# Weights beside the attention land in two half places of their own, and the local branch's table of distances holds 320 columns

## The chip, the cores and the metric

The kernel runs on one core of one Trainium2 chip. The metric is the device time of one execution in microseconds (us). The kernel before took 1309.75 us (median of 3 runs, 1309.35 to 1310.75).

The core's engines have the names that the profile gives them: PE is TensorE (matmuls; PEld is its weight loads), DVE is VectorE, ACT is ScalarE, POOL is GpSimd, and SP issues the DMAs. Every engine works through its own list of instructions in order and waits on semaphores.

## The reference

One decoder layer over 1024 tokens of width 1024, all in float32. A joint projection of x feeds two groups of heads side by side: four differential heads (two softmaxes of 64-wide queries and keys, the second subtracted with a factor, then an RMS norm) and eight heads of native sparse attention (NSA) over two key groups. Each NSA head adds three gated branches: compressed keys, selected blocks, and a local window of 512. The local branch is what the table of distances belongs to:

```
mask = (dist_i >= 0) & (dist_i < WINDOW) & (kpos >= 0)[None, :]
s = jnp.einsum('bqghd,bkgd->bqghk', q_blk, kblk) * scale
s = s - slopes[None, None, :, :, None] * dist[None, :, None, None, :]
p = masked_softmax(s, mask[None, :, None, None, :])
```

Sixteen blocks are selected of sixteen that there are, so the selected branch is plain causal attention. Behind the attention come the output projection, a layer norm, a SwiGLU feed-forward part (width 2816) and a second layer norm.

## The kernel before, in words

**Precision.** A float32 matrix is split into a rounded part hi and a rest lo (`split`, L79: ACT casts, DVE or POOL subtracts), and a product is three matmuls, hi*hi, hi*lo and lo*hi (`mm3`, L114).

**Stages.** First the keys and the compressed branch's inputs are projected, then the values, then attention runs in units, and beside it the remaining projections run as fillers. Then the output projection ends, and the feed-forward part takes the second half of the span, from about 700 us on. Its code is not touched, but for the pool in which a small tile of statistics lies (L1166).

**Units.** A unit is one block of 128 queries of a pair of NSA heads in one branch (`nsa_units`, L361; kind 0 is the selected branch together with the compressed one, kind 1 the local one) or of one differential head (`diff_units`, L430). Its front computes scores into a psS bank (L311, L312), adds the distances and takes the minimum on DVE (L318), exponentiates on ACT (L332) and scales on POOL (L397, L454). Its back transposes on PE (L351, L341), splits again on ACT and DVE, and multiplies by the values into psO (L412, L414, L467). A front writes into one or two of six t tiles, and they stay taken until the back has read them. Distances come from tables made once on POOL at the start (`masks`, L259): dsel for causal attention, dwin for the local window, dcmp for the compressed keys. A local unit has up to five blocks of keys, 640 columns, reduced in two parts of 320.

**Fillers.** `k_fill`, `q_fill` and `dv_fill` (L511 to L554) each load a weight, split it and run chains of matmuls into one of two psM banks; 24 matmuls of 512 columns make a chain for half of the tokens. A q chain then needs two q tiles of a ring of four, which come free when an earlier half's scores are done; k and v chains write into named slots. The weights sit in a ring of five tiles of 1024 columns (`w_tile`, L69). `load_split` (L85) takes a third tile of this ring for the raw weight. It loads it in two halves of 512 columns, ACT casts each half into hi, and POOL subtracts it into lo (L90, L91).

**Order.** All instructions are written down in the order of the phase table (L783): per phase its units, its fillers, how many units may be open before the oldest one's back is written (look), how fast the fillers are spread, and by how many places a back's priority is put behind (later). Fillers stand 2000 places behind (`FILL_LATER`, L29). A planner then fixes each engine's order: it takes what is ready by a simulated clock and has the best priority, and gives out tiles as they come free in that simulation. The engines follow the fixed order on the chip.

**The end of the attention.** When four blocks of a differential head are done, `finish` (L477) normalises them, transposes them (L486) and stores them to mix_d. The output projection of a row block loads its rows from mix_d (`out_start`, L575), so its second half waits for head 3's finish.

Of the kernel before, what the change touches and what calls it, by code (L numbers as in the profile page):

```python
# [37 lines left out]
def layer_kernel(ctx: ExitStack, tc: tile.TileContext, xT, x, w_t, w_vg, w_dv, lam_in, subln,  # L38
# [105 lines left out]
    with ExitStack() as ctx_a:  # L144
# [105 lines left out]
        dsel = pa.tile([P, 1024], F32, tag="dsel", name="dsel", bufs=1)  # L250
        dwin = pa.tile([P, 640], F32, tag="dwin", name="dwin", bufs=1)
        dcmp = pa.tile([P, NC + 56], F32, tag="dcmp", name="dcmp", bufs=1)
# [6 lines left out]
        def masks():  # L259
# [3 lines left out]
                                    compare_op=ALU.is_ge, fill=BIG)  # L263
            nc.gpsimd.iota(dwin, pattern=[[-1, 640]], base=512, channel_multiplier=1,
                           allow_small_or_imprecise_dtypes=True)
            nc.gpsimd.affine_select(dwin, dwin, pattern=[[-1, 640]], base=512, channel_multiplier=1,
                                    compare_op=ALU.is_ge, fill=BIG)
            nc.gpsimd.affine_select(dwin, dwin, pattern=[[1, 640]], base=-1, channel_multiplier=-1,
                                    compare_op=ALU.is_ge, fill=BIG)
# [30 lines left out]

        def scores(q, k, k0, width, dist, slope, m, t, cmp=None):

            c = NC if cmp else 0
            n = (c + width + 511) // 512
            w = -(-(c + width) // (32 * n)) * 32
            part, at = width - (n - 1) * w, 0
            m0 = None
            for h in range(n):
                ps = ps_s()
                ks = slice(k0 + at, k0 + at + part + c)  # L310
                nc.tensor.matmul(ps[:, :c + part], lhsT=q[0], rhs=k[:, ks], start=True, stop=False)  # L311
                nc.tensor.matmul(ps[:, :c + part], lhsT=q[1], rhs=k[:, ks], start=False, stop=True)  # L312
                if c:
                    k0 += c
                    nc.vector.tensor_tensor_reduce(out=cmp[0], in0=ps[:, :c], in1=cmp[1], scale=slope, scalar=3.0e38,
                                                   op0=ALU.add, op1=ALU.min, accum_out=cmp[2])
                m1 = m if h == n - 1 else pa.tile([P, 1], F32, tag="m0", name="m0", bufs=4)
                nc.vector.tensor_tensor_reduce(out=t[:, at:at + part], in0=ps[:, c:c + part],  # L318
                                               in1=dist[:, at:at + part], scale=slope,
                                               scalar=3.0e38 if h == 0 else m0, op0=ALU.add, op1=ALU.min,  # L320
                                               accum_out=m1)
                at, part, c, m0 = at + part, w, 0, m1
# [38 lines left out]
        def nsa_units(p, qt, K, V):  # L361
# [7 lines left out]
            def make(i, kind):  # L369
# [5 lines left out]
                def front():  # L375
                    dist = dsel[:, 1024 - width:] if kind == 0 else dwin[:, 640 - width:]
                    m = small([P, 4], "m", 4)
# [5 lines left out]
                    for a in range(2):  # L383
                        ms, rs = ([t[:, n:n + 1] for n in (a, 2 + a)] for t in (m, r))
                        cmp = (pc[:, a, :], dcmp[:, 56 - 8 * i:56 - 8 * i + NC], ms[1]) if kind == 0 else None
                        scores(q_of(qt, i, a), K[kind], j0 * P, width, dist, sl[a], ms[0], ts[a], cmp)
                        exps(ts[a], width, ms[0], rs[0])
# [109 lines left out]

        there = set()  # L500
# [10 lines left out]
        def k_fill(n, where, out, halves=(0, 1)):  # L511
            def steps():
                if 0 in halves:
                    out.extend([slot(m) for m in where])
                    out.append(load_split(w_t[n], *w_tiles(), l_eng="pool", pieces=2))
                for hf in halves:
# [7 lines left out]
        def q_fill(n, hf, qt, tiles=w_tiles):  # L524

            def steps():
                if hf == 0:
                    qt.append(load_split(w_t[n], *tiles(), l_eng="pool", pieces=2))
                w = qt[0]
# [11 lines left out]
        def dv_fill(pair, where, out, blocks, tiles):  # L541
            def steps():
                if pair not in dv_parts:
                    dv_parts[pair] = [(*load_split(w_dv[pair, :, kk, :], *tiles(kk), l_eng="pool", pieces=2), 4 * kk, 4)
                                      for kk in range(2)]
# [226 lines left out]
        def held_fill():  # L772

            def steps():
# [12 lines left out]
             [qf(1, 1), wo_copy(0), dvf(0, range(8)), qf(2, 0)], 2, 1.25, 80),  # L787
            ([(nsa, 2, range(8))],
             [qf(2, 1), kdf(0, 0), wo_copy(1), qf(3, 0), kdf(0, 1)], 2, 1.25, 60),
            ([(nsa, 3, (1, 0, 2, 3, 5, 4, 6, 7))],  # L790
             [qf(3, 1), qdf(0, 0), kdf(1, 0), kdf(1, 1)], 2, 1.25, 60),
            ([(diff, 0, (2, 1, 0, 3, 5, 4, 6, 7))],
# [7 lines left out]
            ([(diff, 2, (4, 7, 6, 5))],  # L800
             [wo_fill(0), qdf(3, 1), wo_fill(1), held_fill(), out_fill(0, False), out_fill(1, False)], 2, 1.25, 20),
            ([(diff, 3, range(4, 8))],
             [ln_fill((0, 1)), out_fill(2, True), out_fill(3, True)], 2, 0.9, 60),
# [357 lines left out]
    for j in range(4):  # L1161
# [3 lines left out]
        nc.vector.tensor_add(acc[j + 4][:, LO], acc[j + 4][:, LO], us[j])  # L1165
        s = const.tile([P, 3, 6], F32, tag="st3", name="st3", bufs=4)[:, :3 if j == 3 else 2, :]  # L1166
        nc.vector.bn_stats(s[:, s.shape[1] - 1, :], acc[j + 4][:, HI])
# [79 lines left out]
```

## Time and profile before

| | us |
|---|---|
| median of the runs (lowest to highest) | 1309.75 (1309.35 to 1310.75) |
| the profiled execution | 1310.08 |
| its span, first to last instruction | 1308.3 |
| PE busy (share of the span) | 1289.5 (99%) |
| PEld busy | 1107.7 (85%) |
| DVE busy | 912.5 (70%) |
| ACT busy | 649.2 (50%) |
| POOL busy | 464.6 (36%) |

The profiled execution's time is 1.8 us longer than its span. Matmuls are pipelined, and their ends are modelled, so a busy PE can still be waiting a little between two matmuls. The granted clock of TensorE is 1.00 of full speed in every stretch shown.

### The profile page before, as it was taken

How to read it: one execution, taken by the hardware profiler on the slowest of the kernel's cores; microseconds unless marked ns; L12 is line 12 of the kernel's file. 1: busy time of each engine (PE TensorE's matmuls, PEld its weight loads, DVE VectorE, ACT ScalarE, POOL GpSimd, SP SyncE). 2: the span in 40 equal slices, each digit the busy share in tenths (PEclk: the TensorE clock that was granted, in tenths of full speed). 3: DMA queues.
4: the chain of work that ended last, by engine and by line, in shares of the span. 5: the costliest groups of instructions: out<-in, count | busy, mean ns of one | idle time of the engine just before them, and what ended most of it. 6: DMA issues, size and time to landing. Idle time of an engine off the chain costs nothing.

```text
span 1308.3 us, 20482 instructions
## 1 busy us (share of the span) xinstructions
PE 1289.5 (99%) x6955; PEld 1107.7 (85%) x6955; DVE 912.5 (70%) x1956; ACT 649.2 (50%) x1398; POOL 464.6 (36%) x499
## 2 busy tenths in 40 slices
PE   9999999999999999999999999999999999999997
PEld 7898998888899889788887888888888888888886
DVE  5537758778788666773787677776767768555588
ACT  5337667778777566652344333333233335543330
POOL 4515354355545446633623313232231322000071
PEclk9999999999999999999999999999999999999999
DMA  9411022121213126632214566655555549768641
GB/s 356 144 27 49 22 61 49 31 66 23 56 42 71 49 65 162 210 104 98 97 59 141 202 220 232 194 169 176 184 159 196 185 171 338 271 199 289 196 169 65
DMA packets 86841, 183.13 MB, mean 140 GB/s; under 512 B 10576, under 2 KB 19152, under 8 KB 86608
## 3 DMA queue, kind: packets, MB, share of 16 engines
q1 hardware_dynamic: 86736, 181.82, 42.9%
q8 instruction: 55, 0.90, 0.3%
q14 instruction: 50, 0.41, 0.1%
HBM read 116.18 MB, written 57.15 MB: 132 GB/s over the span
## 4 chain that ended last, share of the span: by engine, by line
PE 93%; DVE 4%; ACT 2%; issue 1%; DMA 0%; POOL 0%; SPq 0%; DVEq 0%; ACTq 0%
PE psM L116 11%; PE psM L117 11%; PE psM L118 11%; PE psT L116 6%; PE psT L117 6%; PE psT L118 6%; PE psS L118 6%; PE psS L117 6%; PE psS L116 6%; PE psT L351 4%; PE psS L311 3%; PE psS L312 3%; PE psO L414 2%; PE psO L467 2%; PE psO L412 2%; PE psO L117 2%
## 5 line engine op out<-in xcount | busy, mean ns | idle before, releaser
L332 ACT ACTIVATE t<-t,m 128x384 f32<-128x384 f32 (+7 forms) x192 | 144.2, 752 | 56.2 <-DVE m L318 53.3
L397 POOL TENSOR_SCALAR t<-t,r,gates 128x640 f32<-128x640 f32 (+7 forms) x128 | 100.3, 790 | 190.3 <-DVE r L391 101.0
L116 PE MATMUL psM<-big,w 128*128 128x512 f32 x304 | 121.2, 399 | 1.0 <-ACT w L81 0.6
L118 PE MATMUL psM<-big,w 128*128 128x512 f32 x304 | 120.1, 396 | 0.0
L117 PE MATMUL psM<-big,w 128*128 128x512 f32 x304 | 119.6, 394 | 0.0
L311 PE MATMUL psS<-slot,q 128*128 128x320 f32 (+10 forms) x304 | 111.6, 369 | 2.1 <-DVE m L318 1.8
L995 POOL TENSOR_TENSOR half<-half,half 128x512 f32<-128x512 f32 x22 | 33.1, 1506 | 204.9 <-ACT half L994 204.9
L312 PE MATMUL psS<-slot,q 128*128 128x320 f32 (+10 forms) x304 | 99.3, 329 | 0.0
L83 DVE TENSOR_TENSOR pt<-psT,pt 128x512 fp32r<-128x512 f32 (+1 forms) x152 | 91.0, 612 | 8.4 <-ACT pt L81 7.6
L83 DVE TENSOR_TENSOR op<-op 128x1024 fp32r<-128x1024 f32 x44 | 60.1, 1374 | 37.9 <-ACT op L81 37.2
L81 ACT CAST big<-slot 128x1024 fp32r<-128x1024 f32 (+1 forms) x54 | 54.4, 1018 | 63.7 <-DVE slot L987 50.6
L351 PE MATMUL psT<-ident,t 128*128 128x128 f32 x528 | 84.1, 273 | 0.4 <-DVE pt L83 0.2
L81 ACT CAST pt<-psT 128x512 fp32r<-128x512 f32 (+1 forms) x152 | 76.5, 525 | 16.1 <-PE psT L351 11.1
L83 DVE TENSOR_TENSOR big<-slot,big 128x1024 fp32r<-128x1024 f32 (+1 forms) x54 | 63.9, 1191 | 27.6 <-ACT big L81 27.6
L81 ACT CAST op<-op 128x1024 fp32r<-128x1024 f32 x44 | 45.8, 1050 | 63.4 <-DMA op<-t_d 61.3
L414 PE MATMUL psO<-pt,slot 128*128 128x256 f32 x264 | 73.0, 298 | 1.0 <-DVE pt L83 0.6
L999 POOL TENSOR_TENSOR half<-half,half 128x512 f32<-128x512 f32 x22 | 36.5, 1661 | 100.0 <-DVE half L998 99.8
L412 PE MATMUL psO<-pt,slot 128*128 128x256 f32 x264 | 71.5, 288 | 0.0
L318 DVE CUSTOM_DVE_ANT_0 t<-psS,dsel 128x384 f32<-128x384 f32 (+9 forms) x128 | 62.6, 493 | 11.7 <-PE psS L312 9.8
L116 PEld LDWEIGHTS psM<-big,w 128*128 128x128 f32 x304 | 57.1, 188 | 13.5 <-ACT w L81 1.3
L118 PEld LDWEIGHTS psM<-big,w 128*128 128x128 f32 x304 | 57.1, 188 | 11.2
L81 ACT CAST big<-big 128x1024 fp32r<-128x1024 f32 (+1 forms) x49 | 44.3, 911 | 44.6 <-DMA big<-t_d 36.0
(370 smaller groups left out, 3965.9 us busy)
## 6 DMA issues: line engine op xcount, KB each, us to landing
a_d<-slot SPq DMA_DIRECT2D x77, 256.0 KB, 3.0
t_d<-slot SPq DMA_DIRECT2D x77, 256.0 KB, 2.2
q<-q SPq DMA_DIRECT2D x48, 256.0 KB, 3.0
slot<-in_w_up_dram SPq DMA_DIRECT2D x22, 512.0 KB, 3.7
slot<-in_w_down_dram SPq DMA_DIRECT2D x22, 512.0 KB, 3.8
op<-a_d SPq DMA_DIRECT2D x44, 256.0 KB, 3.9
op<-t_d SPq DMA_DIRECT2D x44, 256.0 KB, 4.6
big<-a_d SPq DMA_DIRECT2D x33, 256.0 KB, 3.5
```

Source lines behind the costliest of these rows:

```text
L81: nc.scalar.copy(hi, src)
L83: eng.tensor_sub(lo, src, hi.bitcast(F32))
L116: nc.tensor.matmul(acc, lhsT=ah, rhs=bh, start=first, stop=False, skip_group_check=more)
L117: nc.tensor.matmul(acc, lhsT=ah, rhs=bl, start=False, stop=False, skip_group_check=more)
L118: nc.tensor.matmul(acc, lhsT=al, rhs=bh, start=False, stop=last, skip_group_check=more)
L311: nc.tensor.matmul(ps[:, :c + part], lhsT=q[0], rhs=k[:, ks], start=True, stop=False)
L312: nc.tensor.matmul(ps[:, :c + part], lhsT=q[1], rhs=k[:, ks], start=False, stop=True)
L332: nc.scalar.activation(t[:, :width], t[:, :width], AF.Exp, bias=m, scale=-1.0, accum_out=r)
L351: nc.tensor.transpose(tp[:rows, n * P:(n + 1) * P], s, ident)
L397: nc.gpsimd.tensor_scalar(t, t, r[:, c:c + 1], gates[:, i, gc:gc + 1], op0=ALU.mult, op1=ALU.mult)
L412: nc.tensor.matmul(po[:, :256], lhsT=v, rhs=pt[:, 0, n * 256:(n + 1) * 256], start=False, stop=False)
L414: nc.tensor.matmul(po[:, :256], lhsT=v, rhs=pt[:, 1, n * 256:(n + 1) * 256], start=False, stop=last)
```

## The change

Five things are changed.

- `load_weights` is new and takes the place of `load_split` in the three fillers. The raw weight lands in two tiles of 512 columns with a tag of their own (raw, two of them), one for each half, and not in the ring of five; casts and subtractions are as before.
- dwin holds 320 columns instead of 640. It is read only for the first part of a full local unit (five blocks); the second part, and local units of fewer blocks, read dsel. One of two affine_select instructions for dwin goes.
- In the phase table the last block of head pair 2 moves from its own phase into the next one, and that phase puts backs 200 places behind instead of 60.
- In the last phase but one, three units are open instead of two, and backs are put 40 places behind instead of 20. In the last phase head 3's blocks come in the order 5, 4, 6, 7.
- The small statistics tiles st3 of the last stage lie in another pool.

```
-        dwin = pa.tile([P, 640], F32, tag="dwin", name="dwin", bufs=1)
+        dwin = pa.tile([P, 320], F32, tag="dwin", name="dwin", bufs=1)
...
-            nc.gpsimd.iota(dwin, pattern=[[-1, 640]], base=512, channel_multiplier=1,
+            nc.gpsimd.iota(dwin, pattern=[[-1, 320]], base=512, channel_multiplier=1,
                            allow_small_or_imprecise_dtypes=True)
-            nc.gpsimd.affine_select(dwin, dwin, pattern=[[-1, 640]], base=512, channel_multiplier=1,
-                                    compare_op=ALU.is_ge, fill=BIG)
-            nc.gpsimd.affine_select(dwin, dwin, pattern=[[1, 640]], base=-1, channel_multiplier=-1,
+            nc.gpsimd.affine_select(dwin, dwin, pattern=[[1, 320]], base=-1, channel_multiplier=-1,
                                     compare_op=ALU.is_ge, fill=BIG)
...
-                                               in1=dist[:, at:at + part], scale=slope,
+                                               in1=(dist if h or first is None else first)[:, at:at + part], scale=slope,
...
-                    dist = dsel[:, 1024 - width:] if kind == 0 else dwin[:, 640 - width:]
+                    dist = dsel[:, 1024 - width:]
+                    first = dwin if kind and nb == WIN_BLOCKS else None
...
+        def load_weights(src, hi, lo):
+            for k in range(2):
+                cs = slice(k * 512, (k + 1) * 512)
+                raw = pa.tile([P, 512], F32, tag="raw", name="raw", bufs=2)
+                nc.sync.dma_start(raw, src[:, cs])
+                split(raw, hi[:, cs], lo[:, cs], "pool")
+            return hi, lo
...
-                    out.append(load_split(w_t[n], *w_tiles(), l_eng="pool", pieces=2))
+                    out.append(load_weights(w_t[n], *w_tiles()))
...
-                    qt.append(load_split(w_t[n], *tiles(), l_eng="pool", pieces=2))
+                    qt.append(load_weights(w_t[n], *tiles()))
...
-                    dv_parts[pair] = [(*load_split(w_dv[pair, :, kk, :], *tiles(kk), l_eng="pool", pieces=2), 4 * kk, 4)
+                    dv_parts[pair] = [(*load_weights(w_dv[pair, :, kk, :], *tiles(kk)), 4 * kk, 4)
...
-            ([(nsa, 2, range(8))],
+            ([(nsa, 2, range(7))],
              [qf(2, 1), kdf(0, 0), wo_copy(1), qf(3, 0), kdf(0, 1)], 2, 1.25, 60),
-            ([(nsa, 3, (1, 0, 2, 3, 5, 4, 6, 7))],
-             [qf(3, 1), qdf(0, 0), kdf(1, 0), kdf(1, 1)], 2, 1.25, 60),
+            ([(nsa, 2, (7,)), (nsa, 3, (1, 0, 2, 3, 5, 4, 6, 7))],
+             [qf(3, 1), qdf(0, 0), kdf(1, 0), kdf(1, 1)], 2, 1.25, 200),
...
-             [wo_fill(0), qdf(3, 1), wo_fill(1), held_fill(), out_fill(0, False), out_fill(1, False)], 2, 1.25, 20),
-            ([(diff, 3, range(4, 8))],
+             [wo_fill(0), qdf(3, 1), wo_fill(1), held_fill(), out_fill(0, False), out_fill(1, False)], 3, 1.25, 40),
+            ([(diff, 3, (5, 4, 6, 7))],
...
-        s = const.tile([P, 3, 6], F32, tag="st3", name="st3", bufs=4)[:, :3 if j == 3 else 2, :]
+        s = pb.tile([P, 3, 6], F32, tag="st3", name="st3", bufs=4)[:, :3 if j == 3 else 2, :]
```

## Rows read from the trace of the kernel before

**Rows 1.** The page's busy times: engine, us, share of the span, instructions.

```profile
PE 1289.5 (99%) x6955; PEld 1107.7 (85%) x6955; DVE 912.5 (70%) x1956; ACT 649.2 (50%) x1398; POOL 464.6 (36%) x499
```

**Rows 2.** Chosen stretches: length, engines' busy us (instructions), granted clock, DMA share, GB/s.

```profile
60.00:700.00 640.00, 631.24 (x3978) 560.09 (x3977) 456.47 (x1400) 403.16 (x1073) 288.30 (x345) 1.00 0.25 73
...
200.00:244.00 44.00, 43.08 (x294) 38.17 (x294) 39.21 (x138) 36.42 (x94) 17.39 (x25) 1.00 0.17 40
...
288.00:320.00 32.00, 31.32 (x230) 28.15 (x229) 30.27 (x104) 26.97 (x66) 13.33 (x18) 1.00 0.04 10
...
368.00:412.00 44.00, 43.02 (x324) 40.19 (x323) 42.10 (x145) 38.76 (x100) 20.11 (x29) 1.00 0.14 31
...
532.00:560.00 28.00, 25.85 (x163) 21.96 (x162) 21.60 (x63) 21.97 (x53) 21.15 (x19) 1.00 0.62 189
```

**Rows 3.** The same stretches, tile psM alone (PE, PEld, DVE, ACT).

```profile
200.00:244.00 44.00, 6.19 (x24) 4.35 (x24) 1.43 (x2) 1.96 (x3) 1.00 0.17 40
...
288.00:320.00 32.00, 0.52 (x3) 0.09 (x1) 0.00 (x0) 0.00 (x0) 1.00 0.04 10
```

**Rows 4.** Groups of PE instructions by form: busy us, mean ns, idle before.

```profile
L116 PE MATMUL psM<-big,w 128*128 128x512 f32 x304 | 121.2, 399 | 1.0 <-ACT w L81 0.6 <-DVE slot L171 0.3
...
L116 PE MATMUL psT<-big 128*128 128x512 f32 x112 | 43.6, 389 | 0.0
```

**Rows 5.** POOL in order of time, 0 to 24 us: start us, us, instruction.

```profile
5.64 0.71 POOL L266 TENSOR_SCALAR_AFFINE_SELECT dwin<-dwin 128x640 f32<-128x640 f32 x1
...
8.61 1.03 POOL L268 TENSOR_SCALAR_AFFINE_SELECT dwin<-dwin 128x640 f32<-128x640 f32 x1
...
11.72 1.42 POOL L83 TENSOR_TENSOR w<-slot,w 128x512 fp32r<-128x512 f32 x1 [1.49 <-DMA slot<-in_w_t_dram]
```

**Rows 6.** Groups of DVE's score reductions by form, 84 to 560 us.

```profile
L318 DVE CUSTOM_DVE_ANT_0 t<-psS,dwin,m 128x320 f32<-128x320 f32 x32 | 17.3, 539 | 6.0 <-PE psS L312 5.8
...
L318 DVE CUSTOM_DVE_ANT_0 t<-psS,dsel,m 128x320 f32<-128x320 f32 x8 | 4.4, 549 | 0.5 <-PE psS L312 0.4
...
L318 DVE CUSTOM_DVE_ANT_0 t<-psS,dsel,m 128x448 f32<-128x448 f32 x6 | 4.1, 680 | 1.6 <-PE psS L312 1.4
```

**Rows 7.** Groups of ring-tile casts and subtractions by form, 84 to 560 us.

```profile
L81 ACT CAST w<-w 128x512 fp32r<-128x512 f32 x28 | 16.5, 622 | 10.2 <-DMA w<-in_w_t_dram 5.3 <-DMA w<-in_w_dv_dram 1.6 <-PE psM L117 1.3
...
L83 POOL TENSOR_TENSOR w<-w 128x512 fp32r<-128x512 f32 x24 | 30.6, 1294 | 9.5 <-ACT w L81 9.5
```

**Rows 8.** DMAs that line 90 issues, 12 to 500 us: time to landing.

```profile
DMA to landing us min/median/max: 2.6/3.4/10.2
```

**Rows 9.** SP's queue in order of time, 196 to 206 us.

```profile
200.94 1.21 SPq L90 DMA_DIRECT2D w<-in_w_t_dram  x2
```

**Rows 10.** Stretches, instructions on ring tile w alone (PE, PEld, DVE, ACT, POOL).

```profile
204.00:261.00 57.00, 17.05 (x70) 12.52 (x69) 0.00 (x0) 0.00 (x0) 0.00 (x0) 1.00 0.17 36
261.00:268.00 7.00, 1.18 (x6) 0.68 (x5) 0.00 (x0) 1.15 (x2) 2.54 (x2) 1.00 0.05 14
...
276.00:282.00 6.00, 0.96 (x4) 0.83 (x5) 0.00 (x0) 1.15 (x2) 2.55 (x2) 1.00 0.30 96
```

**Rows 11.** Stretches of 6 us around four hand-overs, all instructions.

```profile
112.00:118.00 6.00, 5.75 (x36) 4.73 (x34) 5.06 (x18) 5.90 (x15) 4.62 (x6) 1.00 0.05 12
...
275.00:281.00 6.00, 5.79 (x38) 4.61 (x36) 5.27 (x18) 5.93 (x17) 3.71 (x5) 1.00 0.14 37
344.00:350.00 6.00, 5.62 (x37) 4.53 (x36) 5.44 (x22) 5.90 (x17) 3.82 (x4) 1.00 0.06 16
...
484.00:490.00 6.00, 5.71 (x37) 4.91 (x36) 4.09 (x10) 5.34 (x12) 2.53 (x2) 1.00 0.21 66
```

**Rows 12.** Waits, 532 to 560 us: who for whom, us, times, longest.

```profile
PEld psO L467 <- ACT ms L472: 2.0, 3, 0.9
```

**Rows 13.** PE in order of time, 551 to 552.3 us.

```profile
551.85 0.63 PE L486 MATMUL psT<-ident,od 128*128 128x128 f32 x4 [1.08 <-DVE r L449]
```

**Rows 14.** Instructions on tile q, 196 to 246 us: ns min/median/max, first and last start.

```profile
L176 ACT ACTIVATE q<-psM,qscale x2: 691/694/696, 201.4 to 242.7; 128x512 fp32r<-128x512 f32 x2
```

More of the change, by code (lines that the diff above doesn't have):

```diff
@@ L299, in q_of, with scores @@
             return q[:, c:c + P], q[:, 512 + c:512 + c + P]
-        def scores(q, k, k0, width, dist, slope, m, t, cmp=None):
+        def scores(q, k, k0, width, dist, slope, m, t, cmp=None, first=None):
             c = NC if cmp else 0
@@ L385, in front @@
                         cmp = (pc[:, a, :], dcmp[:, 56 - 8 * i:56 - 8 * i + NC], ms[1]) if kind == 0 else None
-                        scores(q_of(qt, i, a), K[kind], j0 * P, width, dist, sl[a], ms[0], ts[a], cmp)
+                        scores(q_of(qt, i, a), K[kind], j0 * P, width, dist, sl[a], ms[0], ts[a], cmp, first)
                         exps(ts[a], width, ms[0], rs[0])
```

## The prediction

> **What bounds the kernel now.** I read four views in this order. The page's busy times first: TensorE (PE) is busy for 1289.5 us of a span of 1308.3, while VectorE (DVE) has 912.5, ScalarE 649.2 and GpSimd (POOL) 464.6 [rows 1]. All matmuls of the kernel before stay, so the change can only win or lose PE's idle time, and the reader should look for where that lies. The second view, the busy time of each engine in chosen stretches, places it. The stretch that the diff can reach, from the projections to the start of the feed-forward part (60 to 700 us), holds PE for 631.24 of 640 us, so 8.8 us of visible idle time. Three stretches of the block-sparse heads (200:244, 288:320, 368:412) have 0.92, 0.68 and 0.98 us of it; the stretch where the two last differential heads meet the output projection (532:560) has 2.15 us [rows 2]. In the first three DVE is busy for 39.21 of 44, 30.27 of 32 and 42.10 of 44 us: these stretches are held by DVE's score and evacuation work, and PE waits in small steps.
>
> The third view, the same stretches for the tile psM alone, says why: psM holds the filler matmuls (projections put in beside attention), and the first two of these stretches have 24 and 3 of them (24 make one chain) among 294 and 230 matmuls [rows 2, 3]. PE waits where it has no filler. The fourth view, groups of instructions by form, shows that visible idle time isn't all: the same 128x512 matmul lasts 399 ns on average as filler and 389 ns in the feed-forward part [rows 4]; over 304 of them that is 3.0 us of waiting that counts as busy. So the attention stage has perhaps 12 us to give (8.8 + 3.0, my estimate), and that is the floor of anything said below.
>
> One rule is weighed here. The row gives PE 99% busy [rows 1]. The Trainium skill (Perfetto Trace Analysis, Identifying the Most-Contended Engine) says that matmul busy share is a bad measure of headroom because matmuls are pipelined; the 399 against 389 ns agree with it. By the row alone the most that could be won is 8.8 us, by the rule it is more, 11.8 with the group just named.
>
> **The change part by part.** The sum is made on the profiled execution, 1310.08 us (span 1308.3 and 1.8 around it), which lies 0.33 above the median of the runs, 1309.75.
>
> *The smaller table.* One affine_select of 0.71 us goes, the other (1.03 us) and the iota are halved: 0.71 + 0.51 = 1.2 us less of POOL and a little of the iota, estimated in proportion. All of it lies before 9.7 us, and POOL's first split of a weight at 11.72 us comes after 1.49 us idle behind a DMA [rows 5]. That DMA hides it; were the cover gone, the gain would be 1.2 us. I take 0. Of the 96 score reductions of the local branch, 64 now read dsel where they read dwin (32 of narrow blocks, 32 second parts of full ones). A second part of 320 columns takes 539 ns from dwin and 549 from dsel [rows 6]: 64 x 0.01 = 0.6 us of DVE lost at most, spread over four head pairs, beside PE work. I take 0.
>
> *The landing places.* Each weight is still two DMAs of 512 columns, two ScalarE casts of 622 ns and two GpSimd subtractions of 1294 ns [rows 7]: nothing is added or removed. What moves is what holds a ring tile. Today raw, hi and lo share five tiles: two weights in use hold four, and raw of the next sits in the fifth until both of its results have tiles. The trace shows it: between 204 and 261 us no cast and no subtraction of a ring tile runs, though the two DMAs issued from 200.94 us on land within 3.4 us by the median [rows 8, 9]; their two casts and two subtractions follow in 261:268, once the 70 filler matmuls before have let a weight go [rows 10]. Afterwards the fifth tile is free for hi, so the casts can run before a weight is let go, and only the subtractions stay: a hand-over shrinks from 0.62 + 2 x 1.29 = 3.2 us to 2.6. The new wait is that of a load's DMA on the subtraction of the same half of the load before; behind it in SP's queue stand q moves and stores of mix, and the scores of a unit wait for a q move. I cost that at nothing: a load is wanted long after that subtraction (57 us in the stretch above), and where it isn't, the price is one subtraction, 1.3 us. There are twelve loads beside the attention (24 subtractions [rows 7]). The 6 us around four hand-overs hold visible PE idle time: 0.25, 0.21, 0.38 and 0.29 us [rows 11]. So the upper end is 12 x 0.6 = 7.2 us won; the lower end is 1.2 us lost, two casts that run at a moment when ScalarE, busy 36.42 and 38.76 us of 44 [rows 2], would rather feed attention. I take the idle time of those four, 1.1 us won.
>
> *The phase table of head pairs 2 and 3.* The last block of pair 2 moves into pair 3's phase, and there the value and transpose half of a unit is put 200 instead of 60 places later. Scores run further ahead there, and pair 3's fillers come one block earlier. DVE has 1.9 us idle in 368:412 and PE 0.98 [rows 2]. No row shows this order, so I bound it: won at most the 1.9 us that DVE can still fill; lost as much, if the late halves hold t tiles that the next scores need. I take 1.0 us won, PE's own idle.
>
> *The last two phases.* Heads 2 and 3 now keep three units open instead of two, 40 places later instead of 20, and head 3 begins with block 5. Nearest rows: PE's 2.15 us idle of 532:560 [rows 2], where its weight loads wait 2.0 us for ScalarE's squares and PE 1.08 us for DVE before the transposes of head 3's first four blocks at 551.85 us [rows 12, 13]. A further open unit gives PE scores to do there: at most 2.15 us won. It also puts one more front ahead of head 3's finish: an 896-column front is four score reductions of 448 columns, 4 x 0.68 = 2.7 us of DVE [rows 6], the price if nothing covers it. I take 1.5 us won.
>
> Sum: 0 - 1.1 - 1.0 - 1.5 = -3.6, so 1306.5 by this execution and 1306.1 on the scale of the median.
>
> **Rivals.** *Hidden anyway.* The fillers of the idle stretches are not held by weights but by where they go. In 200:244 two q evacuations run, the first at 201.4 and the second at 242.7 us [rows 14]; psM has two banks, so a result that waits for its q tile holds one, and with both held no further chain can start, whatever weights are ready. For it: 288:320 sees 3 filler matmuls [rows 3], although a weight's casts and subtractions were done in 276:282 [rows 10]. Against it: the phase table changes too. Then the time is 1309.7, give or take 2.
>
> *Much more.* If the ring was what starved those stretches, filler would spread into them and most of the 8.8 us visible and 3.0 hidden would go, but not what lies at 660:700: some 9 us, 1300.7 on the median's scale. The Trainium skill (Perfetto Trace Analysis, Optimization Strategy) says that one gap repeating on the engine that should be saturated can mean too little SBUF or PSUM for the next tile; by that rule this rival holds if the tile is the ring's, and the previous one if it is the PSUM bank's. Against it: the two q evacuations just named.
>
> *Slower.* Three open units delay head 3's finish. The output projection's first rows wait for that finish, so its fillers start later, and 532:560 has nothing else to give PE. Price: 2.7 us for the front ahead, on top of today's idle: 1310.08 + 2.7 = 1312.8, or 1312.5 on the median's scale, and up to twice that if both open heads delay it. It decides from the moment when the transposes of line 486 start more than about 3 us later, relative to the fronts around them, than now.
>
> **How the numbers follow.** Forecast 0.43, much more 0.12, hidden anyway 0.27, slower 0.18. A measurement of this kernel tells about 0.2%, 2.6 us, from no change, so faster means under 1307.1 and slower above 1312.4. The forecast's own spread (bounds 7.2 + 1.9 + 2.15 won against 1.2 + 1.9 + 2.7 + 0.6 lost) leaves 0.35 of its 0.43 below 1307.1; with 0.12, and 0.04 of hidden anyway, that is 0.51. Slower: 0.12 of the last rival, 0.04 of hidden anyway and 0.02 of the forecast, 0.18. The rest, 0.31, is no change. The range goes from 1299.5, which holds most of the case of much more, to 1313.0, which holds half of the last rival; what is left out on both sides is about 0.15.
>
> **What would show it.** Right for the landing places: casts of weights soon after landing, with no stretch like 204:261 without one, and shorter gaps between a weight's last matmul and the next one's subtraction. Right for hidden anyway: the same stretches with 24 or fewer psM matmuls, and q evacuations 40 us apart. For pair 3: less PE idle in the stretch that answers to 368:412. For the last phases: PE idle near the line 486 transposes, now 2.15 us, and the time between the last unit of head 3's first four and those transposes. The prediction is wrong if PE's idle time before the feed-forward part isn't below 7 us, or if the time moves while that idle time doesn't.

## The result: slower

The changed kernel takes 1318.12 us by the median of 5 runs (1316.23 to 1318.57), against 1309.75 before. The ratio is 1.0058 [1.0047, 1.0069], so it is 8.4 us slower. The profiled execution took 1318.57 us and has a span of 1316.8, 8.5 more than before.

The page's busy times after, and then the five chosen stretches, in the columns of [rows 1] and [rows 2]:

```profile
PE 1292.8 (98%) x6955; PEld 1109.3 (84%) x6955; DVE 909.4 (69%) x1956; ACT 650.3 (49%) x1398; POOL 465.5 (35%) x498
```

```profile
60.00:700.00 640.00, 626.10 (x3939) 554.60 (x3939) 445.41 (x1386) 398.79 (x1059) 286.43 (x343) 1.00 0.25 71
200.00:244.00 44.00, 42.35 (x284) 36.70 (x282) 37.75 (x134) 37.10 (x97) 18.48 (x26) 1.00 0.15 33
288.00:320.00 32.00, 31.71 (x229) 28.50 (x227) 29.23 (x103) 27.02 (x67) 13.35 (x18) 1.00 0.08 18
368.00:412.00 44.00, 42.73 (x308) 38.31 (x307) 40.34 (x139) 36.67 (x93) 20.64 (x29) 1.00 0.12 25
532.00:560.00 28.00, 25.52 (x145) 21.41 (x144) 19.57 (x55) 18.03 (x43) 21.26 (x18) 1.00 0.75 235
```

The matmuls are the same in number, and PE's visible idle time from 60 to 700 us is 13.9 us where it was 8.8 [rows 2]. That is 5.1 of the 8.5 us; the rest is busy time. Three of the four stretches that were to gain lost: 1.65 us idle in 200:244 (0.92 before), 1.27 in 368:412 (0.98), 2.48 in 532:560 (2.15). The fourth, 288:320, has 0.29 where it had 0.68.

The stretches were chosen for the forecast. A division of the whole stage, before and then after, finds the largest loss outside them:

```profile
60.00:420.00 360.00, 354.92 (x2399) 321.57 (x2398) 262.88 (x951) 255.92 (x727) 157.19 (x224) 1.00 0.18 45
...
480.00:520.00 40.00, 39.71 (x266) 35.98 (x265) 27.29 (x82) 27.50 (x76) 25.83 (x29) 1.00 0.53 139
520.00:560.00 40.00, 37.85 (x241) 32.91 (x240) 28.34 (x87) 27.62 (x71) 24.33 (x24) 1.00 0.62 197
```

```profile
60.00:420.00 360.00, 353.73 (x2373) 317.91 (x2373) 259.31 (x942) 255.90 (x717) 153.52 (x221) 1.00 0.18 43
...
480.00:520.00 40.00, 36.20 (x224) 32.32 (x224) 26.44 (x72) 22.86 (x63) 24.43 (x25) 0.98 0.41 121
520.00:560.00 40.00, 37.52 (x235) 33.21 (x234) 25.38 (x77) 25.04 (x67) 24.22 (x24) 0.98 0.65 189
```

In 480:520 PE is idle for 3.80 us instead of 0.29, and the granted clock of the two late stretches is 0.98. The next view is the last result of the attention work: the last DVE instruction of a block-sparse unit (line 420 before, 421 after) and of a differential unit (471 and 472). The last two figures ahead of the semicolon are first and last start.

```profile
L420 DVE TENSOR_TENSOR tmp<-psO,tmp x32: 384/410/418, 107.2 to 414.3; 64x256 f32<-64x256 f32 x32
L471 DVE COPY od<-psO x27: 270/291/292, 441.0 to 604.9; 128x128 f32<-128x128 f32 x27
```

```profile
L421 DVE TENSOR_TENSOR tmp<-psO,tmp x32: 384/414/417, 104.9 to 417.4; 64x256 f32<-64x256 f32 x32
L472 DVE COPY od<-psO x27: 275/292/293, 445.3 to 612.2; 128x128 f32<-128x128 f32 x27
```

The block-sparse heads end 3.1 us later and all attention 7.3 us later. More filler doesn't account for it. From the start of the span to the end of the block-sparse heads psM has 738 matmuls in both kernels; to the end of all attention it has these (in the columns of [rows 3]), before and after:

```profile
0.00:604.90 604.90, 274.65 (x1275) 208.74 (x1275) 33.11 (x48) 30.43 (x56) 1.00 0.30 87
```

```profile
0.00:612.20 612.20, 277.17 (x1270) 209.31 (x1270) 32.97 (x48) 30.47 (x56) 1.00 0.30 86
```

So 7.3 of the 8.5 us are attention that comes later over the same filler; the other 1.2 lie behind it.

### The profile page after: what moved, and what is told of

It is laid out like the page before. It is cut to its first block, busy times and chain, and to the rows that moved or that the text cites. A ratio compares the mean times of both kernels' runs of the same rounds, so it can differ in the third digit from the quotient of the medians.

```text
span 1316.8 us, 20474 instructions
## 1 busy us (share of the span) xinstructions
PE 1292.8 (98%) x6955; PEld 1109.3 (84%) x6955; DVE 909.4 (69%) x1956; ACT 650.3 (49%) x1398; POOL 465.5 (35%) x498
## 4 chain that ended last, share of the span: by engine, by line
PE 88%; DVE 5%; issue 2%; DMA 2%; POOL 1%; ACT 1%; SPq 0%; DVEq 0%; ACTq 0%; POOLq 0%
PE psM L116 10%; PE psM L117 10%; PE psM L118 10%; PE psS L118 6%; PE psS L116 6%; PE psS L117 6%; PE psT L116 6%; PE psT L117 6%; PE psT L118 6%; PE psT L351 4%; PE psS L311 3%; PE psS L312 3%; PE psO L415 2%; PE psO L468 2%; PE psO L413 2%
## 5 line engine op out<-in xcount | busy, mean ns | idle before, releaser
L318 DVE CUSTOM_DVE_ANT_0 t<-psS,dsel 128x384 f32<-128x384 f32 (+9 forms) x160 | 77.8, 491 | 22.2 <-PE psS L312 21.0
L318 DVE CUSTOM_DVE_ANT_0 t<-psS,dsel,m 128x320 f32<-128x320 f32 (+7 forms) x112 | 67.3, 601 | 24.5 <-PE psS L312 22.5
L81 ACT CAST pt<-psT 128x512 fp32r<-128x512 f32 (+1 forms) x152 | 77.2, 525 | 13.9 <-PE psT L351 8.9
L311 PEld LDWEIGHTS psS<-slot,q 128*128 128x128 f32 x304 | 57.4, 189 | 14.9 <-DVE m L318 6.0
L116 PEld LDWEIGHTS psM<-big,w 128*128 128x128 f32 x304 | 57.2, 188 | 11.8 <-DVE q L177 0.9
```

The costliest lines, as they stand in the source:

```text
L81: nc.scalar.copy(hi, src)
L116: nc.tensor.matmul(acc, lhsT=ah, rhs=bh, start=first, stop=False, skip_group_check=more)
```

## Three places where it shows

*Filler earlier, then missing.* What the change was to do, it does in part: a weight is cast soon after it lands. ACT in order of time, after:

```profile
181.55 0.62 ACT L81 CAST w<-raw 128x512 fp32r<-128x512 f32 x1 [2.58 <-DMA raw<-in_w_t_dram]
...
186.30 0.62 ACT L81 CAST w<-raw 128x512 fp32r<-128x512 f32 x1 [1.16 <-DMA raw<-in_w_t_dram]
...
201.85 0.62 ACT L81 CAST w<-raw 128x512 fp32r<-128x512 f32 x1
...
267.70 0.62 ACT L81 CAST w<-raw 128x512 fp32r<-128x512 f32 x1
```

But a long stretch without a cast stays: between the last two rows, for 65 us, no raw weight is cast. The two casts that stood in 261:268 before [rows 10] now come some 60 us earlier, and the next one only at 267.70.

The matmuls of psM alone (length; PE's busy us and count; clock, DMA share, GB/s), before and after, show what follows:

```profile
180.00:200.00 20.00, 12.16 (x46) 1.00 0.15 53
193.00:205.00 12.00, 5.18 (x21) 1.00 0.21 61
...
460.00:480.00 20.00, 13.76 (x55) 1.00 0.32 79
480.00:500.00 20.00, 12.32 (x51) 1.00 0.41 131
```

```profile
180.00:200.00 20.00, 8.52 (x32) 1.00 0.28 83
193.00:205.00 12.00, 0.81 (x3) 1.00 0.20 57
...
460.00:480.00 20.00, 14.89 (x61) 1.00 0.33 80
480.00:500.00 20.00, 10.20 (x43) 1.00 0.20 65
```

The chains end sooner, and the next doesn't begin sooner. In 193:205 there are 3 filler matmuls instead of 21. In 460:480 there are 6 more than before and in 480:500 then 8 fewer, for the results of head 3's k leave psM later, not earlier. ACT's half of these evacuations, before and after (two banks, two instructions each):

```profile
481.17 0.58 ACT L170 CAST slot<-psM 64x512 fp32r<-64x512 f32 x1 [0.18 <-PE psS L312]
485.44 0.58 ACT L170 CAST slot<-psM 64x512 fp32r<-64x512 f32 x1
486.63 1.07 ACT L170 CAST slot<-psM 64x512 fp32r<-64x512 f32 x2 [0.17 <-PE psS L312]
```

```profile
488.56 1.06 ACT L170 CAST slot<-psM 64x512 fp32r<-64x512 f32 x2
...
492.23 1.06 ACT L170 CAST slot<-psM 64x512 fp32r<-64x512 f32 x2
```

Before, two of them wait for a score matmul (psS of line 312), which reads such a slot. psM has two banks, so no third chain begins until one is empty.

*A q move on PE's path.* Head 3's first scores, PE in order of time, before and after:

```profile
508.97 0.30 PE L311 MATMUL psS<-slot,q 128*128 128x128 f32 x1
```

```profile
517.40 0.33 PE L311 MATMUL psS<-slot,q 128*128 128x128 f32 x1 [2.79 <-DMA q<-q]
```

The q tile behind it, before and after (ACT's and DVE's evacuation, then the moves in SP's queue):

```profile
500.20 0.71 ACT L176 ACTIVATE q<-psM,qscale 128x512 fp32r<-128x512 f32 x1
...
500.94 0.75 DVE L177 SCALAR_TENSOR_TENSOR q<-psM,qscale,q 128x512 fp32r<-128x512 f32 x1 [0.55 <-ACT q L176]
...
501.72 4.69 SPq L161 DMA_DIRECT2D q<-q  x3
```

```profile
506.63 0.71 ACT L176 ACTIVATE q<-psM,qscale 128x512 fp32r<-128x512 f32 x1
...
509.24 0.74 DVE L177 SCALAR_TENSOR_TENSOR q<-psM,qscale,q 128x512 fp32r<-128x512 f32 x1
...
510.01 1.11 SPq L161 DMA_DIRECT2D q<-q  x2
514.35 0.46 SPq L161 DMA_DIRECT2D q<-q  x1
```

The q is made 6.4 us later, and DVE's half of the evacuation starts 1.9 us after ACT's has ended. The third move, which waits for the first two, is issued at 514.35, and PE waits for it; the chain of three moves itself takes about as long as before (4.8 us against 4.7).

*The granted clock.* Three stretches of 3.2 to 3.4 us in the changed kernel, the first with that wait:

```profile
515.00:518.40 3.40, 1.00 (x8) 1.01 (x9) 0.81 (x5) 0.38 (x2) 0.00 (x0) 1.00 0.90 210
518.40:521.80 3.40, 3.40 (x18) 3.40 (x17) 0.68 (x3) 0.75 (x4) 0.73 (x2) 0.50 0.98 234
521.80:525.00 3.20, 3.20 (x30) 3.20 (x29) 0.90 (x5) 2.49 (x8) 0.00 (x0) 1.00 0.21 49
```

After the idle time the granted clock is 0.50, the lower of its two levels (1.2 of 2.4 GHz), for 3.4 us; PE counts as busy all through. At half speed that is at most 1.7 us more. With the 5.1 us idle it makes 6.8. The last 1.7 of the 8.5 us are a remainder within busy time, some 1.2 of it behind the end of attention; its cause isn't shown.

## The experiments

All ran in rounds beside the kernel before, 4 to 11 executions each, and each ratio is to that kernel.

**One part at a time.** e1_raw has the landing places, the small table and the move of st3, with the old phase table; e2_phases only the new phase table; e5_table only the table and st3.

```
e1:  all lines of after, but the list `phases` of before
e2:  all lines of before, but the list `phases` of after
e5:  before, with dwin of 320 columns, `first`, and st3 in pb
```

> The phase table of before, with the landing places, the table of 320 columns and the st3 tiles of after. Theory L (the landing places cost the time: loads and casts come earlier and push other work): about 1317, near the changed kernel. Theory P (the last phases cost it: three open units delay head 3): 1306 to 1310. Theory O (no part has a price of its own; each edit makes the planner write another order, and single misplacements in it cost or save some us): anywhere from 1305 to 1316, and without the 2.8 us wait of PE for a q move near 517 us only by accident.

> The kernel before with the new phase table alone. Theory L: 1310 or less. Theory P: 1315 or more, with the loss between 484 and 570 us. Theory O: anywhere from 1305 to 1316, and its loss and that of e1_raw don't add up to the 8.4 us of the whole change (they would by either of the others).

> The kernel before with the table of 320 columns and the st3 tiles of after, nothing else; the order of every engine is that of the kernel before. Theory L (the loss of e1_raw is that of the landing places): 1309.5 to 1310.5. If reading dsel in place of dwin costs (64 reductions, 10 ns each, and VectorE bounds the stretches without filler): up to 0.6 us more; if the table were the loss of e1_raw: 1316.

e1: 1316.39 us, 1.0047 [1.0034, 1.0059]. e2: 1313.36, 1.0028 [1.0016, 1.0039]. e5: 1310.14, 1.0000 [0.9992, 1.0009], with every engine's order as before. So the table costs nothing, the landing places some 6 us and the phase table alone some 3, together 9.6 against the 8.4 of the whole change, a difference that the intervals leave open. Were the landing places all of the loss, e2 was to be at 1310 or less, and were it the last phases, at 1315 or more; it is at neither. In e1 PE doesn't wait for a q move between 476 and 640 us (its longest wait there is 1.48 us, for DVE at 491), and it is 6.3 us slower all the same: the landing places cost without that wait.

**The changed kernel with one part of its phase table undone.**

```
e3:  ([(nsa, 2, range(8))], ...  60) and ([(nsa, 3, ...)], ... 60)   as before
e4:  last two phases as before: 2, 1.25, 20  and  (diff, 3, range(4, 8))
```

> The changed kernel with the phases of head pairs 2 and 3 as before. If putting the backs 200 places later costs: 2 to 4 us less than the changed kernel, in 312 to 420 us. Theory P and L: as the changed kernel, 1317 to 1318. Theory O: another time by some us either way, and the stretches before 240 us, which this edit of the table lies behind, as in the changed kernel.

> The changed kernel with the last two phases as before. Theory P: 1310 to 1312. Theory L: 1317 to 1318. Theory O: the wait of 2.8 us for a q move near 517 us stays if the planner's order up to there is the same, since these phases begin behind it; then 1314 to 1318.

e3: 1315.87 us, 1.0045 [1.0032, 1.0058]; e4: 1318.02, 1.0056 [1.0044, 1.0069]. Undoing the last phases gives nothing back. Undoing pairs 2 and 3 gives 2 us by the medians, with intervals that overlap that of the changed kernel.

**The fifth tile held.** e6 is e1 with a small GpSimd copy that takes a ring tile at 41.2 us, and another that frees it at 500.4 us, so that up to there a weight's high half waits again although raw has its own place.

```
 spare = w_tile(F32)
 nc.gpsimd.tensor_copy(spare[:, 0:8], K[0][1][:, 0:8].bitcast(F32))
 ...
+[wo_fill(0), spare_end, qdf(3, 1), ...
```

> The kernel of e1_raw (landing places, table, old phases) with one tile of the ring of five held by a small copy from about 50 us until 490 us. Four tiles are left: a weight's hi gets a tile only when an earlier weight is let go, as in the kernel before, while raw still lands in its own places. Theory E (the free fifth tile is what costs: casts and with them whole filler chains run earlier, and the stretches without filler get longer): 1309 to 1312. Theory Q (the loads from the landing places block SP's queue, so q moves issue 2 to 3 us late): 1315 to 1317 as e1_raw.

1315.79 us, 1.0040 [1.0028, 1.0052]. The total hardly moves; by itself it is what the other theory expected, that loads into the landing places make q moves late. But the trace splits it. The end of the block-sparse heads and of all attention, and two stretches, in e6:

```profile
L421 DVE TENSOR_TENSOR tmp<-psO,tmp x32: 392/410/417, 105.1 to 413.2; 64x256 f32<-64x256 f32 x32
L472 DVE COPY od<-psO x27: 273/291/293, 440.3 to 610.9; 128x128 f32<-128x128 f32 x27
```

```profile
60.00:420.00 360.00, 355.25 (x2397) 321.22 (x2397) 261.86 (x945) 255.20 (x720) 155.38 (x223) 1.00 0.19 45
...
480.00:520.00 40.00, 35.87 (x217) 32.41 (x215) 25.27 (x71) 23.64 (x63) 25.14 (x27) 0.92 0.48 132
```

In e1 the block-sparse heads end at 417.5 us; with the tile held at 413.2, 1.1 us earlier than before the change, and psM has 738 matmuls up to there in both. So up to 420 us the free fifth tile is the cause, and this is shown. By which path it costs is not shown: from 84 to 180 us psM has 314 matmuls in e1 and in e6, and 292 before, so filler that comes earlier there isn't by itself the loss. The gain is lost again after 480 us: PE waits 3.13 us for the same q move, and the clock falls for 6.8 us. That isn't a load in the way of the move: the last one into a landing place is issued at 470.0 us, and the last subtraction that reads one starts at 486.1.

**Free the places that filler waits for.** e7 has five q tiles instead of four; e9 evacuates a q chain into one staging tile and issues its four moves from there.

```
e7:  return pa.tile([P, 1024], F32R, tag="q", name="q", bufs=5)
e9:  both = pa.tile([P, 1024], F32R, tag="both", ...)   # then four moves to the q tiles
```

> The kernel of e5_table with five q tiles instead of four, in the space that the landing places would take. If fillers are held by where they go (a finished q chain keeps its psM bank until a q tile is free): the bank comes free earlier, filler runs in the stretches that have none, and the time falls by 2 to 6 us, to 1304 to 1308. If weights hold them: 1310, no change. If fillers that run earlier are missing later: 1311 to 1316.

> The kernel of e5_table where a q chain's result goes into one staging tile and from there by four moves at once into both q tiles, instead of into the first q tile and on by three moves of which the third waits for two. From evacuation to the last landing 5 to 6 us instead of 9 to 10, and the psM bank needs no q tile to come free. If fillers are held by where they go: 1302 to 1307. If what counts is only that filler is there late: 1310 to 1316.

e7: 1318.21 us, 1.0059 [1.0047, 1.0071]; e9: 1328.94, 1.0141 [1.0128, 1.0154]. Both have the old landing of weights and are slower than any theory had them (1316 at most). With e7 the theory that a place for the results would help falls; e9 says less, for its staging tile is itself waited for:

```profile
131.09 0.38 PE L116 MATMUL psM<-w,big 128*128 128x256 f32 x1 [3.71 <-DVE both L178]
```

e17 spends the landing places' space on a seventh t tile instead (`bufs=7`).

> The kernel before with the table of 320 columns and st3 moved (e5), no landing places, and the space spent on a seventh t tile instead (the tile that holds a unit's scores). If the score tiles limit how far scores run ahead of the rest, the short waits of TensorE in the stretches without filler shrink: up to 3 us, 1307, and the version beats both kernels. If the order written by the planner was settled on six tiles and any release of a resource only moves filler, as with five q tiles: 1313 to 1318. No change (1310) if nothing waits for a t tile.

1315.16 us, 1.0037 [1.0023, 1.0051]: slower too. The Trainium skill (Perfetto Trace Analysis, Optimization Strategy) says that a repeating gap on the engine that should be saturated can mean too few buffers for the next tile. No gain came of it here: with a fifth q tile the time was 1318.21 us, with a seventh t tile 1315.16.

**Make head 3's q earlier.** e10 is the changed kernel with this edit, e19 is e1 with it, and e16 is e19 with a ring tile to be held as in e6.

```
-[kdf(3, 0), kdf(3, 1), qdf(3, 0)], 2, 1.25, 130),
+[kdf(3, 0), qdf(3, 0), kdf(3, 1)], 2, 1.25, 130),
```

> The changed kernel with one edit: in the first half of differential head 2, the first half of head 3's q is projected before the second half of its k. Theory of the late q move: in the changed kernel TensorE waits 2.79 us at 517 us for the third move of head 3's first q tile, after which its granted clock is 0.5 for 3.4 us (1.4 us more). With the q made one chain earlier (5.2 us or more) both must be gone: 1314 us, 4 less than the changed kernel, ratio to the kernel before about 1.003, and the rest of the loss (the filler that runs too early before 440 us) stays. If the wait only moves to another unit or another q tile, or if it was slack that something else uses: 1317 to 1319, no change.

> Landing places, table and st3 with the phase table of before (e1), and the same swap of head 3's q and k halves. Theory of the late q move: e1 waits 1.65 and 0.78 us for q tiles at 491 and 493 us with 3.4 us at the granted clock 0.5 after them; these belong to the same q moves of head 3, so about 3 us go: 1313.5. If the waits at 491 to 493 have another cause (the order of DVE's evacuation): no change, 1316.

> e19 with one ring tile held by a small GpSimd copy from about 50 us until head 2's fillers begin, so that up to there a weight's high half has to wait as in the kernel before. If the two causes (fillers too early before 440 us, about 3 us; late q move and the clock after it, about 3 to 4 us) are the whole loss and add, this kernel comes back to the kernel before: 1310 to 1311, ratio 1.000 to 1.001. If one of them is not a cause: 1313 or more; if a third is at work (subtractions in SP's queue, DVE's order after 500 us): 1313 to 1316 with neither early filler nor the wait at 517 in its trace.

e10: 1316.99 us, 1.0056 [1.0043, 1.0068]; e19: 1318.73, 1.0066 [1.0053, 1.0079]. The wait for the move shrinks to 1.46 us in e10 and the clock holds, but PE now waits 1.77 us at 488 us for DVE and loses 2.04 us in 560:600. The theory that this wait is the rest of the loss falls. (e19 was expected to gain from waits of e1 for q tiles at 491 and 493 us; e1's trace has 1.48 us for DVE and 0.61 for ACT there.) e16 (1320.9 us, 1.0079 [1.0067, 1.0092]) didn't meet its own condition. Its two copies stand 0.3 us apart (41.8 and 42.1 us), so nothing was held, and it says nothing on whether the two causes add.

**Fill the hole after 480 us.** Blocks of the value projection, whose place is free, come between the halves of head 3's k: two of them in e1 (e20), in e6 (e22) and in e5 (e23), three in e1 (e21). With two:

```
-[kdf(3, 0), kdf(3, 1), qdf(3, 0)]        [qdf(2, 1), dvf(1, range(4, 8))]
+[kdf(3, 0), dvf(1, range(4, 6)), kdf(3, 1), qdf(3, 0)]   [..., dvf(1, range(6, 8))]
```

> e1 (landing places with the phase table of before) with one edit: two blocks of the value projection of the second head pair, which stood one phase later, are put between the two halves of head 3's k. Theory of the held banks: in e1 both psM banks hold finished halves of that k from 486 us until head 1's last scores free their slots, and no filler runs until 497 us (10.9 us; 4.1 us in the kernel before); the short waits of TensorE beyond the streaming of its matmuls come to 4.8 us in 480 to 520 (1.1 before). The blocks have a free destination, so 5 us of filler fill the hole: 2 to 3 us less, 1313.5 to 1314.5. If the hole is only where lost time shows, and the attention work sets it: 1316 or more.

> The same with three blocks (7.8 us of filler). Theory of the held banks: the rest of the hole goes too, 1313; but the first q of head 3 is made one block later, and TensorE may wait for its moves as at 517 us in the changed kernel (3 us): then 1316. If the attention work sets it: 1316 or more.

> e6 (one ring tile held up to 500 us, so that the fillers before 440 us run as late as in the kernel before) with the two blocks. If fillers that run too early before 440 us (3 us) and the hole after 480 us (3 us) are the two causes and add: 1311 to 1312, nearly the kernel before. If the second isn't a cause: 1316, as e6.

> The kernel before with the small table only (e5, 1310.1) and the two blocks. Its hole is 4.1 us long and costs TensorE about 0.5 us: the edit has little to fill, 1309 to 1310.5 by the theory of the held banks. If any shift of filler against the attention work costs some us, whatever it fills: 1313 or more.

e20: 1317.12 us, 1.0055 [1.0041, 1.0069]; e21: 1325.85, 1.0123 [1.0109, 1.0137]; e22: 1320.41, 1.0083 [1.0070, 1.0097]; e23: 1315.25, 1.0041 [1.0029, 1.0054]. e22 lies above both times that were expected of it (1311 to 1312, or 1316). e23 has no landing places, has a short hole to fill, and loses 5 us, as expected if any shift of filler costs. The most telling pair of traces is e1 and then e20.

```profile
480.00:520.00 40.00, 37.90 (x230) 33.38 (x229) 27.67 (x77) 24.72 (x67) 25.90 (x26) 0.96 0.44 127
520.00:560.00 40.00, 37.12 (x238) 32.48 (x237) 26.52 (x78) 24.98 (x68) 23.79 (x23) 1.00 0.61 184
```

```profile
480.00:520.00 40.00, 40.00 (x264) 36.33 (x264) 23.90 (x66) 25.78 (x67) 21.98 (x23) 1.00 0.38 115
520.00:560.00 40.00, 35.09 (x206) 29.03 (x204) 28.16 (x92) 24.91 (x69) 25.88 (x26) 1.00 0.64 196
```

The hole is filled: no idle time and full clock in 480:520. But 520:560 loses 4.91 us instead of 2.88, and the two together have 4.91 where they had 4.98. Filler is a fixed stock, and what fills one hole is missing in the next: psM has 133 matmuls instead of 108 in 480:520, and 82 instead of 109 in 520:560.

**Move the late halves of four units.** e6 with 100 or 160 places in place of 130.

> e6 (landing places, one ring tile held up to 500 us) with the value and transpose half of the units of head 2's first half put 100 instead of 130 places later. Its order of instructions around head 1's last units and head 3's first is a little nearer to that of the kernel before than e6's. Theory that the rest of the loss is the order in which the last sixteen units come (19.2 us from the end of head 1 to that of head 2's fourth unit before, 25.9 in e6): some of it comes back, 1311 to 1314. If that stretch is long for a reason that the order doesn't hold, the landing places themselves or their waits: 1315 to 1317 as e6.

> The same with 160 places; its order there lies further from that of the kernel before. By the theory of the order the time moves, up or down by 2 us or more against e6, with the end of head 2's fourth unit; by the theory of the landing places' own waits it stays at 1315 to 1317.

e24: 1314.99 us, 1.0037 [1.0025, 1.0050]; e25: 1316.81, 1.0046 [1.0033, 1.0060]; e6 had 1315.79. The differences are within the spread of the runs, and the two theories stay untold apart. But e24 and e6 make a close pair for the clock. First scores of head 3 and the time around them, e6 and then e24:

```profile
514.17 0.48 PE L311 MATMUL psS<-slot,q 128*128 128x128 f32 x1 [3.13 <-DMA q<-q]
```

```profile
513.80:520.60 6.80, 6.43 (x30) 6.43 (x31) 1.28 (x7) 1.18 (x5) 0.72 (x2) 0.50 0.70 181
```

```profile
515.05 0.33 PE L311 MATMUL psS<-slot,q 128*128 128x128 f32 x1 [3.18 <-DMA q<-q]
```

```profile
515.10:518.50 3.40, 3.40 (x30) 3.40 (x30) 1.21 (x7) 0.88 (x4) 0.73 (x2) 1.00 0.88 254
```

The same wait came before a clock of 0.50 for 6.8 us in one execution and none in the other: 30 matmuls, nearly the same ones in the same order, took 6.43 us or 3.40.

## Why the prediction was wrong

*The premise: too narrow.* It said that the change can only win or lose PE's idle time. Of the 8.5 us lost 5.1 are idle time; the rest is in busy time, and the half-speed stretch is at most 1.7 of it.

*The table: right.* Taken at 0, measured at 1.0000 [0.9992, 1.0009] (e5).

*The landing places: this step failed.* It took 1.1 us won, with bounds from 7.2 won to 1.2 lost; e1 lost 6.3 (1316.39 against 1310.09). What it said of the casts held in part: they come soon after landing, but its sign, no stretch like 204:261 without one, fails (none from 201.85 to 267.70). What it took from that failed: it summed idle time around four hand-overs, as though filler that can start sooner were a gain wherever it starts. The filler is a stock of fixed size beside attention work of fixed size, so an earlier start adds none. With the tile held, and the high halves waiting again, the block-sparse heads are back at their old time. That this waiting helps by keeping filler back for the stretches where PE has nothing else is argued, not shown. The lower end of the bounds counted two casts at a bad moment and never an attention stage that ends 7 us later. The wait costed at nothing, a DMA on the subtraction of the load before, isn't what cost up to 420 us: e6 has that wait too and the block-sparse heads end as early as before. Behind 490 us nothing loads or reads a landing place any more.

*Head pairs 2 and 3: not won.* 1.0 us was taken as won. With the new phase table alone (e2) the block-sparse heads end at 416.0 us, 1.7 later than before. Beside the landing places, undoing this part leaves them at 417.8 (417.4 with it) and gives 2 us in all, by medians alone.

*The last two phases: 1.5 taken as won, not seen.* e4 without them has the time of the changed kernel, and in 532:560, where the gain was to come, PE is idle for 2.34 us in e4 and for 2.48 with them. The transposes of line 486 (487 after) stand at 560.32 us and wait 0.98 us for DVE, as they had 1.08 before [rows 13]: the third open unit hasn't filled that wait.

*The rivals.* "Slower" came out in sign, but its mechanism, three open units delaying head 3's finish, is not the cause, since e4 undoes it for nothing. "Hidden anyway" rested on results that find no place. Its signs came: 24 psM matmuls in 200:244 as before, q evacuations at 203.4 and 244.8 us, 3 filler matmuls in 193:205. But the change wasn't neutral. "Much more" falls with e1. The test that was set, idle time before the feed-forward part below 7 us, fails at 13.9.

*What stays open.* Up to 420 us the cause is shown, by holding the tile. After 480 us it is not: with the tile held, attention starts its last part 1.1 us early and ends 6.0 us late (610.9 against 604.9). A wait for a q move with a fall of the clock, and a hole in the filler, stand there; taking either away by another order lost the time elsewhere (e10, e20). The landing places are out of use by 490 us, so what they cost later comes, as far as the traces tell, through the order of the instructions and not through a wait for them. No run gives the landing places with the order of before in that part, so whether it is that order alone is argued and not shown. That four kernels without landing places, but with some other change of space or order (e2, e7, e17, e23), lost 3 to 8 us speaks for it (e9, which lost 19, also waits for its staging tile). No version beat the kernel before.

## What to carry to other kernels

Before loading or casting filler's inputs earlier, ask what its chains will wait for next and which stretch will be without them; a resource that seems late may be what paces a fixed stock of work. Count idle time over the whole stage and look at when the work that sets its end is done, for a filled hole in one stretch can be the hole of the next. Where a planner writes the order, time the largest part alone first: here e1 told in one run what a sum of small terms had hidden.

## What the hardware did that was not expected

PE idle for 2.79 us at 517 us was followed by 3.4 us at the lower clock level, and for 3.13 us in e6 by 6.8 us of it, while 3.18 us in e24 and 2.99 us in e4 were followed by none. After a wait of 1.48 us in e1 (at 491 us) the clock was 0.51 for 3.4 us; after 1.46 in e10 it stayed at 1.00. The length of the wait alone doesn't tell whether the clock falls. The five executions of e24 have spans of 1312.4 us where the mean granted clock is 0.999 and up to 1314.4 where it is 0.997, so a single profile of such a kernel can be some 2 us off; that the clock makes all of this difference isn't shown.
